# An encoder trunk whose even layer is done in two parts: seven-product pairs into DRAM, then Fourier stage and attention between the gates

## The chip, the cores and the metric

The kernel runs on one core of a Trainium2 chip. The metric is the device time of one execution in microseconds (us); smaller is better. The engines named below are PE (TensorE, matmul), DVE (VectorE), ACT (ScalarE), POOL (GpSimd) and SP (SyncE, which issues the DMAs).

## What is computed

Two requests (256 and 512 tokens, together 768) go through two layers of width 2048 in fp32. The change is in the even layer:

```python
def _even_layer(x, g, w_in, w_out, q_gain, k_gain, sink, w_f, b_f, rel_bias):
    z = _rmsnorm(x, g) @ w_in
    q, k, v, f, ga, gf = _split(z, EVEN_SPLITS)   # 1536, 512, 512, 512, 1536, 512 columns
    q = _rmsnorm(q.reshape(B, S, N_HEADS, HEAD_DIM), q_gain)       # 12 heads of 128
    k = _rmsnorm(k.reshape(B, S, N_KV_HEADS, HEAD_DIM), k_gain)    # 4 heads of 128
    v = v.reshape(B, S, N_KV_HEADS, HEAD_DIM)
    a = _window_attention(q, k, v, rel_bias, sink) * jax.nn.silu(ga)
    fo = _fourier(f.reshape(B, S, N_FOURIER, FOURIER_DIM), w_f, b_f).reshape(B, S, FOURIER_WIDTH) * jax.nn.silu(gf)
    return x + jnp.concatenate([a, fo], axis=-1) @ w_out
```

The attention sees 128-query blocks against the block before, itself and the block after; two blocks of the first request and four of the second, each with 3 query heads to one key head, make 6 units per group and 4 groups. The Fourier part is the real part of a 2-D DFT over positions and the 128 channels of a group, then a 128x128 map per group. The odd layer (short convolution and spatial gate) is not touched.

## The kernel before

All activations are kept transposed: channels on 128 partitions, the 768 tokens along the free axis, as two halves of 384. An fp32 matrix product is made from three products of high and low parts (fp32r): `three` issues hi·hi, hi·lo and lo·hi, and `split` makes the parts, a cast on ACT (line 131) and a subtraction on DVE (line 132). Inputs stand in SBUF as slots, one pair (hi, lo) per 128 channels and half.

A **block** is 128 output channels for all tokens: 16 input tiles x 2 halves x 3 = 96 matmuls of 384 columns. A **wide** step is the other way round: tokens are the output partitions and 512 output channels the columns, 288 matmuls of 512 columns for all of F. A **seven-product pair** (`strassen`) makes two blocks at once with seven half-sized products, 7 x 24 = 168 matmuls instead of 192; it needs sums of input tiles (`build_sums`) and sums of weights (lines 196 to 202, DVE), and adds results up from PSUM on DVE (lines 498 to 510). The odd layer and both output projections already use it; the even layer's input projection does not.

The even layer before: F wide; the four GF blocks (the gates of the Fourier part) with the Fourier stage between them; then four times K, three Q, V and three GA blocks (attention gates). `qk_norm` normalises a Q or K block on the spot (its sum of squares over channels is a product with a matrix of ones); the six attention units of a group (`attend`) run among the group's V and GA blocks at the times `STARTS`. At the end `load_cat` brings the 16 results back into the slots, and `Out` starts: two duos of plain blocks while the sums are built, then pairs.

PE's order is written by hand: the generators are stepped by a `Pipe` whose clock counts matmul columns, and a generator that yields a number is taken up again when that much of PE's work has been put behind it; `flush` takes up all that is left, at once and in order. The order on the other engines is the framework's, from its own estimate of times. SP's queue is in order like every engine's: a DMA that waits for its buffer holds back those behind it. `row_tile` hands out buffers of 768 columns; `Weights.ahead` loads weights (`wr`, 512 KB) some way ahead and splits them into `wh` and `wl`.

## Time and profile before

| | us |
|---|---|
| median of three runs (2163.90 to 2166.14) | 2164.87 |
| the profiled execution | 2162.2 |
| its span, first to last instruction | 2160.4 |
| PE busy in it | 2120.9 |
| F wide: 5.4 to | 89.6 |
| GF blocks and Fourier stage: to | 195.8 |
| four groups of K, Q, V, GA: to | 802.7 |
| output projection of the even layer: to | 1052.7 |

Stage ends are those of their last matmuls on PE. The four groups take 156.9 us each. The span is read with PE in mind: it is busy 98% of it, so a matmul that goes away shortens the run by its pitch, and a wait that is put on PE lengthens it.

### The profile page before, as it was taken

To read this page: it belongs to the slowest core of one execution; us is meant where nothing else is said; L and a number is where in the kernel's file an instruction comes from. 1 tells how busy PE (TensorE), PEld (TensorE's weight loads), DVE (VectorE), ACT (ScalarE), POOL (GpSimd) and SP (SyncE) were. 2 spreads that over 40 slices of the span, in tenths; PEclk is the share of its full clock that TensorE was granted. 3 is DMA by queue.
4 is the path that set the end of the run, shared out by engine and by line. 5 is a ranking of instruction groups with operands and counts; after the bars stand their busy time and mean duration, and the time that the engine had idled before them with its cause. 6 is when DMAs were issued, how large, how long until landed. Compare 5 with 4: busy or idle time off the path is not lost.

```text
span 2160.4 us, 31653 instructions
## 1 busy us (share of the span) xinstructions
PE 2120.9 (98%) x12034; PEld 2074.6 (96%) x12034; DVE 1429.5 (66%) x2466; ACT 898.9 (42%) x1761; POOL 75.0 (3%) x75
## 2 busy tenths in 40 slices
PE   7999999999999998999899999999999999999999
PEld 5899999999999998999888999999999999999999
DVE  8535755745746768666795666666666777796665
ACT  6323443443444464333544433333334554553332
POOL 5000000000000000122100000000000000000000
PEclk9999999999999999999999999999999999999999
DMA  6522112122122148344946322222222332494342
GB/s 220 145 71 77 59 65 76 50 75 66 59 66 76 49 158 275 109 137 137 312 169 194 114 72 86 86 86 76 76 76 86 105 105 97 132 305 153 119 135 74
DMA packets 116512, 250.03 MB, mean 116 GB/s; under 512 B 12636, under 2 KB 72200, under 8 KB 116360
## 3 DMA queue, kind: packets, MB, share of 16 engines
q1 hardware_dynamic: 116360, 248.01, 35.3%
q8 instruction: 94, 1.54, 0.3%
q14 instruction: 58, 0.48, 0.1%
HBM read 210.19 MB, written 40.91 MB: 116 GB/s over the span
## 4 chain that ended last, share of the span: by engine, by line
PE 90%; DVE 3%; DMA 3%; ACT 2%; issue 1%; SPq 0%; DVEq 0%; ACTq 0%
PE bank L117 89%; DMA slot<-cat 1%; PE bank L127 1%; DMA xr<-in_x_t_dram 1%; DMA s<-slot 1%; DVE slot L268 1%; DVE slot L132 1%; DVE wl L132 0%; ACT sc L730 0%; DVE slot L395 0%; DVE slot L397 0%; ACT L730 0%; ACT L350 0%; DVE slot L396 0%; DVE slot L394 0%
## 5 line engine op out<-in xcount | busy, mean ns | idle before, releaser
L117 PE MATMUL bank<-slot,wh 128*128 128x384 f32 x6848 | 1747.0, 336 | 1.3 <-DVE ev L504 1.2
L117 PEld LDWEIGHTS bank<-slot,wh 128*128 128x128 f32 x6848 | 1236.1, 188 | 2.1 <-issue 1.5
L117 PE MATMUL bank<-slot,wl 128*128 128x384 f32 x3424 | 1150.0, 336 | 8.3 <-DVE wl L132 8.3
L131 ACT CAST wh<-wr 128x512 fp32r<-128x512 f32 x728 | 447.9, 620 | 875.8 <-PE bank L117 698.7
L132 DVE TENSOR_TENSOR wl<-wr,wh 128x512 fp32r<-128x512 f32 x728 | 504.8, 697 | 364.2 <-ACT wh L131 351.5
L117 PEld LDWEIGHTS bank<-slot,wl 128*128 128x128 f32 x3424 | 643.4, 188 | 9.6 <-DVE wl L132 9.6
L117 PE MATMUL bank<-wh,slot 128*128 128x512 f32 x576 | 187.1, 403 | 11.3 <-DVE slot L268 5.9
L117 PEld LDWEIGHTS bank<-wh,slot 128*128 128x128 f32 x576 | 111.0, 193 | 37.8 <-DVE slot L268 7.6
L131 ACT CAST slot<-slot 128x384 fp32r<-128x384 f32 x176 | 87.2, 512 | 108.0 <-DVE slot L132 37.4
L132 DVE TENSOR_TENSOR slot<-slot,slot 128x384 fp32r<-128x384 f32 x176 | 97.3, 557 | 31.9 <-ACT slot L131 24.3
L117 PE MATMUL bank<-wl,slot 128*128 128x512 f32 x288 | 115.3, 401 | 1.1 <-DVE wl L132 1.1
L689 DVE RECIPROCAL nrt<-nrt 128x384 f32<-128x384 f32 x32 | 81.6, 2549 | 4.8 <-ACT nrt L688 4.8
L117 PEld LDWEIGHTS bank<-wl,slot 128*128 128x128 f32 x288 | 55.7, 193 | 13.7 <-DVE wl L132 1.6
L345 DVE TENSOR_TENSOR row<-bank,rr 128x384 f32<-128x384 f32 x40 | 22.3, 557 | 39.6 <-PE bank L117 39.6
L200 DVE TENSOR_TENSOR wr<-wr 128x1024 f32<-128x1024 f32 x36 | 47.6, 1322 | 1.2
L202 DVE TENSOR_TENSOR wr<-wr 128x1024 f32<-128x1024 f32 x36 | 44.1, 1226 | 1.2
L196 DVE TENSOR_TENSOR wr<-wr 128x1024 f32<-128x1024 f32 x36 | 44.0, 1221 | 0.5
L198 DVE TENSOR_TENSOR wr<-wr 128x1024 f32<-128x1024 f32 x36 | 43.9, 1220 | 0.4
L790 POOL TENSOR_TENSOR rr<-rr,slot 128x384 f32<-128x384 f32 x24 | 35.3, 1473 | 130.2 <-ACT slot L789 130.2
L502 DVE TENSOR_TENSOR ev<-bank,ev 128x384 f32<-128x384 f32 x36 | 20.1, 558 | 28.7 <-PE bank L117 28.7
L507 DVE TENSOR_TENSOR ev<-ev,bank 128x384 f32<-128x384 f32 x36 | 19.9, 554 | 28.6 <-PE bank L117 28.6
L268 DVE SCALAR_TENSOR_TENSOR slot<-xr,sm,slot 128x384 fp32r<-128x384 f32 x32 | 36.5, 1184 | 3.2 <-ACT slot L267 3.2
(170 smaller groups left out, 1391.6 us busy)
## 6 DMA issues: line engine op xcount, KB each, us to landing
wr<-in_w_in_o_dram SPq DMA_DIRECT2D x96, 512.0 KB, 3.7
wr<-in_w_in_e_dram SPq DMA_DIRECT2D x72, 512.0 KB, 3.7
slot<-cat SPq DMA_DIRECT2D x120, 192.0 KB, 4.2
wr<-in_w_out_e_dram SPq DMA_DIRECT2D x32, 512.0 KB, 3.9
wr<-in_w_out_o_dram SPq DMA_DIRECT2D x32, 512.0 KB, 3.9
slot<-x SPq DMA_DIRECT2D x64, 192.0 KB, 4.2
wr<-in_w_sv_dram SPq DMA_DIRECT2D x16, 512.0 KB, 4.6
xr<-in_x_t_dram SPq DMA_DIRECT2D x15, 384.0 KB, 5.5
```

Source lines behind the costliest of these rows:

```text
L117: nc.tensor.matmul(out, lhsT=lhs, rhs=rhs, start=start, stop=stop, skip_group_check=go_on)
L127: nc.tensor.transpose(out=out, in_=in_, identity=ident)
L131: nc.scalar.copy(out=hi, in_=src)
L132: nc.vector.tensor_sub(out=lo, in0=src, in1=hi.bitcast(F32))
L196: nc.vector.tensor_sub(out=w11, in0=w12, in1=w11)
L198: nc.vector.tensor_sub(out=w11, in0=w22, in1=w11)
L200: nc.vector.tensor_sub(out=w12, in0=w22, in1=w12)
L202: nc.vector.tensor_sub(out=w21, in0=w11, in1=w21)
L268: nc.vector.scalar_tensor_tensor(out=lo, in0=src, scalar=g, in1=hi.bitcast(F32), op0=ALU.mult, op1=ALU.subtract)
L345: nc.vector.tensor_mul(out=out[:, SL[s]], in0=z[s], in1=rr[:, SL[s]])
L689: nc.vector.reciprocal(out=rt, in_=rt)
L790: nc.gpsimd.tensor_add(out=rr[:, SL[h]], in0=rr[:, SL[h]], in1=sq)
```

## The change

The even layer is cut in two. **First part:** F wide as before, but its result goes to DRAM (`put_wide`, `f_d`); GF0 and GF1 as a plain duo, while `build_sums` makes the sums of the normalised inputs; V wide (16 steps, `w_vn`) to DRAM (`ve_d`), while the slots are filled with normalised inputs; then nine seven-product pairs: eight of K and Q blocks, one of GF2 and GF3. Their raw results go to DRAM (`qk_d`); the squares of each K or Q half are summed over channels by a matmul with a one-hot matrix (`pick`) into one of 16 rows of a PSUM bank that stays open for all pairs. GF gates go to DRAM too. **Second part:** the root and reciprocal of the 16 rows; the DFT tables and F are loaded (`tables`), the channel products made (`chan_mix`, before in the F stage) and the Fourier stage runs between GA0 and GA1; then 24 attention units at equal distances among GA2 to GA11. A unit loads its q from DRAM and scales it by a product of 48 rows that picks its factor (`sel`, `rstk`); the gates go through DRAM (`ga_d`). Then `load_cat` and `Out` as before, on other banks.

Over the whole program PE has 9924 matmuls of 128x384 instead of 10548, 1152 of 128x512 instead of 864, 32 new ones of 16 rows x 384 in place of 32 with `ones`, 72 new ones of 128x128 and 8 of 128x384 for `sel` (the 8 are among the 9924), and 24 transposes fewer.

```diff
+FIRST_UNIT, UNITS_AT = 14.0, 10.2
...
-        return rows[-1].tile([P, T], F32, name="row", bufs=5)
+        return rows[-1].tile([P, T], F32, name="row", bufs=4)
...
+    pick = const.tile([P, 31], F32R, name="pick")
+    nc.scalar.activation(out=pick, in_=ident[:, 0:31], func=AF.Copy, scale=0.0)
+    nc.scalar.activation(out=pick[:, 15:16], in_=ident[:, 0:1], func=AF.Copy, scale=0.0, bias=1.0)
...
+    norms = [b for g in range(NKV) for b in [K0 + g] + [Q0 + 3 * g + j for j in range(3)]]
+    pairs_in = [tuple(norms[i:i + 2]) for i in range(0, len(norms), 2)] + [(GF0 + 2, GF0 + 3)]
...
+    order += [(w_in_e, 0, GF0 + g, q) for q in range(4) for g in range(2)]
+    order += [(w_vn, "ve", 0, k) for k in KVE]
+    order += [(w_in_e, 0, b, q) for b in pairs_in for q in range(14)]
+    order += [(w_in_e, 0, GA0 + j, q) for j in range(NQ) for q in (QLATE if j == 0 else range(4))]
...
+        pipe.spawn(build_sums(normalised_x, sums, range(KH), 6.0, True), 1.0)
+        duo = (GF0, GF0 + 1)
+        st.duo(duo, (6, 7, 0, 1), None)
+        for g, b in enumerate(duo):
+            for h, z in enumerate(st.take(b)):
+                t = ev()
+                nc.vector.tensor_mul(out=t, in0=z, in1=rr[:, SL[h]])
+                nc.scalar.activation(out=t, in_=t, func=AF.Silu)
+                nc.sync.dma_start(out=gs_d[g][:, SL[h]], in_=t)
+        zv = [bank(t) for t in (2, 3, 4, 5, 0, 1)]
+        for k in KVE:
+            wide_step("ve", 0, k, zv, KVE)
+            fill(k, 0, xe_d[k][:, SL[0]])
+            fill(k, 1, s4d[k] if k < KH else xe_d[k][:, SL[1]])
+        pipe.flush()
...
+            def squares(self, i, h, t):
+                sq = big(0)
+                a, b = sq[0:64, 0:H], sq[0:64, H:T]
+                nc.scalar.activation(out=a, in_=t[0:64], func=AF.Square)
+                nc.scalar.activation(out=b, in_=t[64:P], func=AF.Square)
+                nc.vector.tensor_add(out=a, in0=a, in1=b)
+                st2 = extra(F32R)
+                nc.scalar.copy(out=st2[0:64], in_=a)
+                nc.vector.tensor_sub(out=st2[64:P], in0=a, in1=st2[0:64].bitcast(F32))
+                yield 3.5
+                mm(stat[h], pick[:, 15 - i:31 - i], st2, i + h == 0 if h == 0 else i == 1, i == 15 - h, True)
...
+        lent[0] = True
+        for b in pairs_in:
+            strassen(0, b, sums, ev, Gates() if b[0] >= GF0 else Normed(), (6, 2, 7, 3))
+        pipe.flush()
+        lent[0] = False
+        for k in range(KH):
...
+    def ga_block(j):
+        z = st.block(GA0 + j, QLATE if j == 0 else range(4))
+        g = row_tile()
+        for s in range(2):
+            nc.scalar.activation(out=g[:, SL[s]], in_=z[s], func=AF.Silu)
+        nc.sync.dma_start(out=ga_d[j], in_=g)
...
+        inv = pool.tile([16, T], F32, name="inv")
+        nc.scalar.activation(out=rstk, in_=rr[0:48], func=AF.Copy, scale=0.0)
+        for s in range(2):
+            nc.scalar.activation(out=inv[:, SL[s]], in_=stat[s], func=AF.Sqrt, bias=eps[0:16], scale=1.0 / P)
+        nc.vector.reciprocal(out=inv, in_=inv)
+        nc.scalar.copy(out=rstk[0:16], in_=inv)
+        nc.vector.tensor_sub(out=rstk[32:48], in0=inv, in1=rstk[0:16].bitcast(F32))
+
+        cwh = pool.tile([P, NF, 2 * P], F32R, name="cwh")
+        cwl = pool.tile([P, NF, 2 * P], F32R, name="cwl")
+        wf = row_tile()[:, :512]
+        nc.sync.dma_start(out=wf.rearrange("c (g d) -> c g d", g=NF), in_=w_f.rearrange("g c d -> c g d"))
+        ch = row_tile()[:, :256]
...
+        def chan_mix():
+            for f in range(NF):
+                ps = bank("s", 2 * P)
+                for j in range(2):
+                    nc.tensor.matmul(ps[:, j * P:(j + 1) * P], lhsT=ch[:, j * P:(j + 1) * P],
+                                     rhs=wf[:, f * P:(f + 1) * P], start=True, stop=True)
+                nc.scalar.copy(out=cwh[:, f, :], in_=ps)
+                nc.vector.tensor_sub(out=cwl[:, f, :], in0=ps, in1=cwh[:, f, :].bitcast(F32))
+                yield 2.0
...
+        def tables():
+            for si in (1, 0):
+                t0, nt = SEQS[si]
+                w, th, tl = tabs[si]
                     raw = row_tile()[:, :2 * w]
-                    nc.sync.dma_start(out=raw, in_=src[t])
+                    nc.sync.dma_start(out=raw, in_=(seq_p, seq_s)[si][t])
                     split(th[:, t, :], tl[:, t, :], raw)
+                    fraw = row_tile()[:, :512]
+                    nc.sync.dma_start(out=fraw, in_=f_d[t0 + t])
+                    split(*ft[t0 + t], fraw)
+                    yield 0.5
...
+        def ungated(g):
+            fo = pool.tile([P, T], F32, name="fo")
+            gf = row_tile()
+            nc.sync.dma_start(out=gf, in_=gs_d[g])
+            yield from fourier(g, fo)
+            gate(gf, NQ + g, fo)
+
+        pipe.spawn(tables(), 1.0)
+        pipe.spawn(chan_mix(), 8.0)
+        for g in range(NF):
+            pipe.spawn(ungated(g), 14.0 + 11.0 * g)
+        for j in range(2):
+            ga_block(j)
+        pipe.flush()
+        rows.pop()
...
+            qr = pool.tile([P, 3 * P], F32, name="qr", bufs=2)
+            nc.sync.dma_start(out=qr.rearrange("p (j c) -> p j c", j=3),
+                              in_=qk_d[4 * g + 1:4 * g + 4, :, t * P:(t + 1) * P].rearrange("j p c -> p j c"))
+            yield 5.0
+            ps = bank("s", 3 * P)
+            for j in range(3):
+                mm(ps[:, j * P:(j + 1) * P], gr.sel[:, j + 1, :], rstk[:, t * P:(t + 1) * P], True, True)
+            q = [pool.tile([P, 3 * P], F32R, name=f"q{e}", bufs=2) for e in "hl"]
+            scaled(qr, qg, ps, *q)
...
+            at = FIRST_UNIT + UNITS_AT * len(units) * g
+            pipe.spawn(gr.load(), max(at - 12.0, 0.0))
+            for i, (s, qb) in enumerate(units):
+                pipe.spawn(attend(gr, s, qb), at - 8.0 + UNITS_AT * i)
+        for j in range(2, NQ):
+            ga_block(j)
+        pipe.flush()
         load_cat([(k, s) for k in range(KT) for s in range(2)])
```

**Loads of tables and F, SP and DVE.** SP's queue at the loads of the DFT tables (`in_seq_p`, `in_seq_s`), in the F stage before; the names in brackets are what a row waits for:

```order
50 L595 DMA row<-in_seq_p_dram 128x260 [waits DMAHW1_49]
51 L595 DMA row<-in_seq_p_dram 128x260 [waits DMAHW2_49]
52 L595 DMA row<-in_seq_s_dram 128x516 [waits DMAHW3_49]
53 L595 DMA row<-in_seq_s_dram 128x516 [waits DMAHW4_49,PE_49]
54 L595 DMA row<-in_seq_s_dram 128x516 [waits DMAHW5_49]
55 L595 DMA row<-in_seq_s_dram 128x516 [waits DMAHW6_49,DMAHW1_49,DVE_49]
56 L184 DMA wr<-in_w_in_e_dram 128x1024 [waits DMAHW7_49]
57 L184 DMA wr<-in_w_in_e_dram 128x1024 [waits DMAHW0_49,DVE_49]
```

and after, where they stand behind the pairs; `f_d` is F, `in_w_in_e` weights:

```order
264 L734 DMA row<-in_seq_s_dram 128x516 [waits DMAHW1_49]
265 L737 DMA row<-f_d 128x512 [waits DMAHW2_49]
266 L734 DMA row<-in_seq_s_dram 128x516 [waits DMAHW3_49,DMAHW1_49,DVE_49]
267 L737 DMA row<-f_d 128x512 [waits DMAHW4_49,DMAHW2_49,DVE_49]
268 L191 DMA wr<-in_w_in_e_dram 128x1024 [waits DMAHW5_49,DVE_49]
269 L734 DMA row<-in_seq_s_dram 128x516 [waits DMAHW6_49,DMAHW3_49,DVE_49]
270 L737 DMA row<-f_d 128x512 [waits DMAHW7_49,DMAHW4_49,DVE_49]
271 L734 DMA row<-in_seq_s_dram 128x516 [waits DMAHW6_49,DMAHW0_49,DVE_49]
272 L737 DMA row<-f_d 128x512 [waits DMAHW7_49,DVE_49]
273 L734 DMA row<-in_seq_p_dram 128x260 [waits DMAHW0_49,DVE_49]
274 L737 DMA row<-f_d 128x512 [waits DMAHW1_49,DVE_49]
```

VectorE there after (`tl` and `fl` are the low parts of tables and F, `inv` the 16 rows' reciprocal):

```order
472 L699 RECIPROCAL inv<-inv 16x768 [waits Activation_49]
473 L134 TENSOR_TENSOR tl_4568<-row,th_4567 128x516 [waits DMAHW1_49,Activation_49]
474 L134 TENSOR_TENSOR fl_4574<-row,fh_4573 128x512 [waits DMAHW2_49,Activation_49]
475 L701 TENSOR_TENSOR rstk<-inv,rstk 16x768 [waits DMAHW5_49,DMAHW4_49,Activation_49]
476 L134 TENSOR_TENSOR wl<-wr,wh 128x512 [waits PE_49] x2
477 L717 TENSOR_TENSOR cwl<-bank,cwh 128x256 [waits PE_49]
478 L717 TENSOR_TENSOR cwl<-bank,cwh 128x256 [waits Activation_49]
479 L134 TENSOR_TENSOR tl_4568<-row,th_4567 128x516 [waits DMAHW3_49,Activation_49]
480 L134 TENSOR_TENSOR fl_4576<-row,fh_4575 128x512 [waits DMAHW4_49,Activation_49]
```

Two loads went out without a wait for DVE; from the third on each load waits for the subtraction that frees its buffer, with the reciprocal ahead of the first.

**Squares of a pair's results, DVE.** Before (`qk_norm`, `sc` is a copy of the bank; line 680 adds the squares):

```order
135 L676 TENSOR_TENSOR sc<-bank,rr 128x384 [waits DMAHW3_49,DMAHW5_49,DMAHW0_49,DMAHW6_49,DVE_49,PE_49]
136 L680 TENSOR_TENSOR sc<-sc,nsq 64x384 [waits Activation_49]
137 L676 TENSOR_TENSOR sc<-bank,rr 128x384 [waits PE_49]
138 L132 TENSOR_TENSOR wl<-wr,wh 128x512 [waits Activation_49]
139 L683 TENSOR_TENSOR pth<-sc,pth 64x384 [waits Activation_49]
140 L680 TENSOR_TENSOR sc<-sc,nsq 64x384 [waits Activation_49]
141 L683 TENSOR_TENSOR pth<-sc,pth 64x384 [waits Activation_49]
```

After, the last two halves of a pair; lines 203, 205 and 207 are sums of weights, 632 and 635 the sum of squares and its low part, 512 a result from PSUM:

```order
226 L203 TENSOR_TENSOR wr<-wr 128x1024 [waits DMAHW3_49,DMAHW2_49,DMAHW5_49,DMAHW1_49,DMAHW6_49,DMAHW0_49,DVE_49]
227 L632 TENSOR_TENSOR big_2181<-big_2181 64x384 [waits Activation_49]
228 L207 TENSOR_TENSOR wr<-wr 128x1024 [waits DMAHW6_49,DVE_49]
229 L635 TENSOR_TENSOR slot_2185<-big_2181,slot_2185 64x384 [waits PE_49,Activation_49]
230 L134 TENSOR_TENSOR wl<-wr,wh 128x512 [waits PE_49]
231 L512 TENSOR_TENSOR ev<-bank,ev 128x384 [waits PE_49]
232 L134 TENSOR_TENSOR wl<-wr,wh 128x512 [waits Activation_49]
233 L205 TENSOR_TENSOR wr<-wr 128x1024 [waits DVE_49]
234 L632 TENSOR_TENSOR big_2224<-big_2224 64x384 [waits Activation_49]
235 L134 TENSOR_TENSOR wl<-wr,wh 128x512 [waits PE_49,Activation_49]
236 L635 TENSOR_TENSOR slot_2228<-big_2224,slot_2228 64x384 [waits Activation_49]
```

What stood in a row among weight splits now stands among sums of weights as well.

**End of the attention, PE.** Before, the last unit's product with V (`pth`, `ptl`) is followed by blocks of the group's gates (`slot`):

```order
4190 L117 MATMUL bank<-slot_339,wh 128x384
4191 L117 MATMUL bank<-slot_338,wl 128x384
4192 L117 MATMUL bank<-pth,vh 128x384
4193 L117 MATMUL bank<-ptl,vh 128x384
4194 L117 MATMUL bank<-pth,vl 128x384
4195 L117 MATMUL bank<-pth,vh 128x384
4196 L117 MATMUL bank<-ptl,vh 128x384
4197 L117 MATMUL bank<-pth,vl 128x384
4198 L117 MATMUL bank<-slot_377,wh 128x384
4199 L117 MATMUL bank<-slot_378,wh 128x384
4200 L117 MATMUL bank<-slot_377,wl 128x384
4201 L117 MATMUL bank<-slot_416,wh 128x384
```

After, in the flush, the last unit's scores:

```order
4031 L119 MATMUL bank<-rstk,sel 128x128 x3
4032 L119 MATMUL bank<-kh,qh 128x256
4033 L119 MATMUL bank<-kl,qh 128x256
4034 L119 MATMUL bank<-kh,ql 128x256
4035 L119 MATMUL bank<-kh,qh 128x256
4036 L119 MATMUL bank<-kl,qh 128x256
4037 L119 MATMUL bank<-kh,ql 128x256
4038 L119 MATMUL bank<-kh,qh 128x256
4039 L119 MATMUL bank<-kl,qh 128x256
4040 L119 MATMUL bank<-kh,ql 128x256
4041 L119 MATMUL bank<-pth,vh 128x384
4042 L119 MATMUL bank<-ptl,vh 128x384
```

and the flush's end, where the `slot` rows are already the output projection's:

```order
4047 L119 MATMUL bank<-pth,vh 128x384
4048 L119 MATMUL bank<-ptl,vh 128x384
4049 L119 MATMUL bank<-pth,vl 128x384
4050 L129 MATMUL bank<-ident,sc 128x128 x6
4051 L119 MATMUL bank<-pth,vh 128x384
4052 L119 MATMUL bank<-ptl,vh 128x384
4053 L119 MATMUL bank<-pth,vl 128x384
4054 L119 MATMUL bank<-pth,vh 128x384
4055 L119 MATMUL bank<-ptl,vh 128x384
4056 L119 MATMUL bank<-pth,vl 128x384
4057 L119 MATMUL bank<-slot_8255,wh 128x384
4058 L119 MATMUL bank<-slot_8256,wh 128x384
```

The rows of three units now stand in a row, with no block between a unit's scores (`kh`, `qh`), its transposes (`ident`) and its product with V.

## Rows read from the trace of the kernel before

**Rows 1.** The page: busy time of each engine, and the chain that ended last.
```profile
PE 2120.9 (98%) x12034; PEld 2074.6 (96%) x12034; DVE 1429.5 (66%) x2466; ACT 898.9 (42%) x1761; POOL 75.0 (3%) x75
PE 90%; DVE 3%; DMA 3%; ACT 2%; issue 1%; SPq 0%; DVEq 0%; ACTq 0%
```

**Rows 2.** What TensorE waited for over the whole span (releaser: total us, times, longest).
```profile
PE bank L117 <- DVE wl L132: 9.4, 5, 3.1
PE bank L561 <- DVE cwl L564: 6.7, 1, 6.7
PE bank L127 <- DVE sc L736: 6.0, 4, 1.5
```

**Rows 3.** Windows: start:end and length, then busy (x count) per engine, clock, DMA share, GB/s.
```profile
1300.00:1400.00 100.00, 100.00 (x577) 100.00 (x576) 63.96 (x98) 32.93 (x57) 0.17 (x3) 1.00 0.26 87
1100.00:1140.00 40.00, 40.00 (x175) 32.47 (x174) 35.92 (x71) 18.12 (x35) 0.00 (x0) 1.00 0.57 197
45.40:52.50 7.10, 0.40 (x3) 0.07 (x1) 7.10 (x7) 3.71 (x8) 4.64 (x3) 0.81 0.29 90
803.00:844.00 41.00, 41.00 (x238) 41.00 (x237) 37.70 (x75) 20.09 (x42) 0.32 (x1) 1.00 0.88 292
```

**Rows 4.** Instructions grouped by line and shape: busy us, mean ns, idle before.
```profile
L131 ACT CAST wh<-wr 128x512 fp32r<-128x512 f32 x728 | 447.9, 620 | 875.8 <-PE bank L117 698.7
L132 DVE TENSOR_TENSOR wl<-wr,wh 128x512 fp32r<-128x512 f32 x728 | 504.8, 697 | 364.2 <-ACT wh L131 351.5
L131 ACT CAST slot<-slot 128x384 fp32r<-128x384 f32 x176 | 87.2, 512 | 108.0 <-DVE slot L132 37.4
L132 DVE TENSOR_TENSOR slot<-slot,slot 128x384 fp32r<-128x384 f32 x176 | 97.3, 557 | 31.9 <-ACT slot L131 24.3 <-DMA s<-slot 5.7
L689 DVE RECIPROCAL nrt<-nrt 128x384 f32<-128x384 f32 x32 | 81.6, 2549 | 4.8 <-ACT nrt L688 4.8
L680 DVE TENSOR_TENSOR sc<-sc,nsq 64x384 f32<-64x384 f32 x32 | 17.6, 550 | 25.6 <-ACT nsq L679 16.1 <-ACT sc L678 9.5
L200 DVE TENSOR_TENSOR wr<-wr 128x1024 f32<-128x1024 f32 x36 | 47.6, 1322 | 1.2
```

**Rows 5.** DMA issues: count, KB each, median us from issue to landing.
```profile
slot<-cat SPq DMA_DIRECT2D x120, 192.0 KB, 4.2
slot<-xhat SPq DMA_DIRECT2D x24, 192.0 KB, 2.5
row<-in_seq_s_dram SPq DMA_DIRECT2D x4, 258.0 KB, 5.2
row<-in_w_f_dram SPq DMA_DIRECT2D x1, 256.0 KB, 3.7
```

**Rows 6.** Timeline of VectorE, one attention unit: scores' end to scaled scores.
```profile
755.13 0.56 DVE L719 CUSTOM_DVE_ANT_0 sc<-bank,bias 128x384 f32<-128x384 f32 x1
756.60 0.17 DVE L727 TENSOR_SCALAR nm<-nm 128x3 f32<-128x3 f32 x1
759.74 0.17 DVE L734 RECIPROCAL den<-den 128x3 f32<-128x3 f32 x1
760.27 1.07 DVE L736 TENSOR_SCALAR sc<-sc,den 128x384 f32<-128x384 f32 x3
```

**Rows 7.** Timeline of TensorE around the channel products of the Fourier branch.
```profile
45.35 0.39 PE L117 MATMUL bank<-wh,slot 128*128 128x512 f32 x1
52.44 1.22 PE L561 MATMUL bank<-row 128*128 128x128 f32 x4 [6.70 <-DVE cwl L564]
53.31 0.77 PE L117 MATMUL bank<-wh,slot 128*128 128x512 f32 x1
```

**Rows 8.** Timeline of ScalarE, a change of activation table and back.
```profile
766.29 0.85 ACT L350 ACTIVATE row<-row 128x768 f32<-128x768 f32 x1
767.14 1.28 ACT L730 ACT_TABLE_LOAD   x1
768.43 0.51 ACT L730 ACTIVATE sc<-sc,nm 128x256 f32<-128x256 f32 x1
```

More of the change, by code (lines that the diff above doesn't have):

```diff
@@ L381, in big, with build_sums @@
     def big(i, dtype=F32):
[L382 to L384 removed]
+        return late[-1].tile([P, PW], dtype, name=f"big{i}")
+    def build_sums(load, sums, order, every, own=False):
         for j in order:
```

483 lines of the change are left out of this document (242 added, 241 removed).

## The prediction

> **What bounds the kernel now.** I read the page first: PE is busy 98% of the span of 2160.4 us and carries 90% of the chain that ended last [rows 1]. So the run is PE's matmuls plus the few places where PE waits, and I need two counts: how many matmuls the change takes away at which pitch, and which waits go or come. The pitch is read from full stretches: in the odd layer's seven-product pairs 577 matmuls of 384 columns in 100 us, 0.174 us each once the two cut by the edges are taken off; in the odd layer's wide step 175 of 512 columns in 40 us, 0.231 [rows 3]. Narrower ones I take in proportion, 0.045 per 100 columns, as an estimate. The waits of PE in the part that changes are few: 6.7 us at the channel products in the F stage, 6.0 in four waits of transposes for scaled scores (the last unit of each of the four groups), and the larger part of 9.4 for weight splits, in the first duos of the output projection [rows 2]. The profiled execution took 2162.2, its span 2160.4; the median of the runs, 2164.87, is 2.7 above it. I make the sum against the profiled one and put it on the median.
>
> **What goes.** Nine pairs by seven products save 9 x 24 = 216 matmuls: -37.6. V as a wide step is 288 x 0.231 = 66.5 for 384 x 0.174 = 66.8: -0.3. 24 transposes fewer, -1.4. The 32 sums of squares with 16 rows stand for 32 with ones: nothing. Scaling q and k by products adds 72 x 0.058 + 8 x 0.174 = +5.6. PE's own work: -33.7.
>
> Three waits go too. In the F stage PE stood from 45.74 to 52.44 for the channel products [rows 7] while VectorE was busy 7.10 of 7.10 us [rows 3], then ran on at a clock of 0.81 in that stretch; they now stand elsewhere. 6.7, the last product's own 0.87 (52.44 to 53.31), and 0.8 for matmuls at the low clock behind it: -8.4 (-6, if the inputs' own splits are late next, to -10). The four waits for scaled scores: -6.0; the tails they stood in no longer exist. In the output projection the weight splits waited because VectorE, 37.7 of 41 us busy there [rows 3], still had to split the 16 results; after the change most of those splits fall into the wait that I find below, so I take -4 of the 6 us of that place (0 to -6). In all -52.1.
>
> **What comes, the Fourier stage.** `row_tile` has four buffers here; `w_f` and `chan` hold two until the channel products are done, so tables and F have one pair of buffers, and six pairs of loads go through it one after another, each waiting for the subtraction of the pair before, as SP's rows show. A turn is a load of 3.7 us (256 KB, little else in flight), a cast 0.62 and a subtraction 0.70 [rows 4, 5]: 5.05 with the hand-over. The first turn ends late: on VectorE the reciprocal of 768 columns, 2 x 2.55 = 5.1 [rows 4], stands ahead of its subtractions, and ahead of that the eight refills of slots, which can be loaded only when the last pair has read them, 4.2 for a load and 8 x 0.56 for the subtractions [rows 4, 5], with a root and its table load on ScalarE some 10.2 us after the last pair's end. So the reciprocal ends at 15.3, the first turn at 16.7, the sixth at 16.7 + 5 x 5.05 = 42. PE comes to the first Fourier product after some 16 us of GA0 and would need 3.6 for its 30 products; it is held until 42: **+22** (16 if a load takes the 2.5 us that the lightest of its kind, `xhat`, took, 29 if it takes the 5.2 that `seq_s` took in a crowded stretch [rows 5]). All of GA0 and GA1 stands behind in PE's queue, so nothing covers it. The fourth Fourier piece runs in the flush, +1.
>
> The Trainium skill, "DMA: Bandwidth & Descriptors", section "Anatomy of one DMA", puts a transfer at 2.0 us plus its bytes at 436 GB/s, 2.6 for 256 KB; by that five turns would cost 5 us less. The rows have 3.7 for this size on SP's queue, and I go by them.
>
> **What comes, the tail of the attention.** After GA11's last matmul a softmax is running and three units have not scored. Their chain is laid bare: from the last score to scaled scores 5.7 us in the trace (755.69 to 761.34 [rows 6]); transposes 1, cast and subtraction 1.1, product with V 1.6. I walked the queues from that matmul: first unit's transposes at 1.9 (slot refills stand between on VectorE); the second scores till 5.6, its q being split first; ScalarE then has eight casts for refills, 8 x 0.51 [rows 4], a copy, a weight cast and a table load ahead of the exponentials, so it is scaled at 14.8; the third's q is cast behind those exponentials, it scores till 15.0 and is scaled at 22.2; PE's order has the second unit's product with V behind the third's transposes, 24.8, and the factors for the last unit's q behind that, so it scores till 27.8, is scaled at 31.6 and done at 34. PE has 13.2 us of work in it: **+21** (14 to 25).
>
> The Trainium skill, "ScalarE: Activation LUTs", section "What ACT_TABLE_LOAD costs", counts 1.28 us and a drain of 1.38 for a switch; two of them here would make the tail 2.8 longer. In the trace the next ACTIVATE starts 0.01 us after the load's 1.28 and the load right at the end of the one before [rows 8], so no drain is added.
>
> **What comes, small waits.** A pair's squares: two adds from PSUM, two squares, an add, a cast and a subtraction, some 4.6 us by durations of 0.5 to 0.56 each [rows 4], for a matmul put 3.5 us of the Pipe's clock (4.3 us by the pitch and the tick) behind; with a weight sum in the way it is late for some halves: +3 (0 to 12). Duo and V with VectorE about 80% busy and 290 GB/s of DMA: the stretch 803 to 844 ran at 92% and 292 GB/s without a wait [rows 3]: +1 (0 to 8). Attention between the gates: a unit of three blocks has 7.0 us for a chain of 5.7 to 7.2: +3 (0 to 10). Matmuls at the low clock behind the two long waits: the one after 6.7 us was 0.57 us from its successor instead of 0.23 [rows 7] and a few like it, in five or six places: +3.
>
> The sum: -52.1 + 22 + 1 + 21 + 3 + 1 + 3 + 3 = +1.9, 2164.1 for the profiled execution, 2166 or 2167 for a median. I say **2166**: what PE saves in matmuls it gives back in two waits.
>
> **The rivals.** *The two waits are half as long.* For it: both hang on queue orders that I walked by hand, loads have been seen at 2.5 us [rows 5], and refills land in any order; against it, SP's rows leave no second buffer. Turns of 4 us, near the 2.5, give 37 instead of 42 (-5), a tail without the refills' casts ahead of the exponentials 26 (-8), and small waits of 5 instead of 10: 2148. By the skill's price for a transfer the first of these alone would hold, 2161. Without either wait it would be 2121, which the orders exclude almost wholly.
>
> *The squares hold up every pair* (slower). For it: two sums of weights of 1.3 us [rows 4] stand among the squares on VectorE, and the stat matmul stands in PE's queue with the pair's products behind it. It decides from a chain of 4.3 us on: with one sum ahead it is 5.9, a wait of 1.6; twice in each of eight pairs is 25 instead of 3, and the chance of once is as large: 2178 to 2188. Against it, `qk_norm` before, with the same 3.5 but without the two adds in front, shows no wait in [rows 2].
>
> *Loads crowd the Fourier stage* (slower): turns of 6.5 give 49, +7, and units in the attention wait 0.4 each, +7: 2180.
>
> *The seven products save nothing* since VectorE becomes the bound in the pairs: it was 64% busy in the odd layer's pairs with PE full [rows 3]; the squares add some 5 points. Under 3%.
>
> **How the numbers follow.** Forecast 40% (its own range 2157 to 2175), half-length waits 27%, squares 16%, crowded loads 14%, others 3%. A measurement of this kernel tells some 0.2%, 4.3 us, from no change: faster means below 2160.5, slower above 2169.2. The first rival gives 27 and the forecast's low end 8: 35% faster. The forecast's high end gives 9, the slow rivals 28: 37% slower. The rest, 28%, is the same. For 8 in 10 the range takes in the first rival's price and most of the slow ones: 2147 to 2184.
>
> **What would show it.** In the profile after: F's last matmul near 81; PE full in the pairs, with small waits for the subtraction of the squares; a wait of some 22 us at the first Fourier product, released by casts and subtractions of tables and F in turn, 5 us apart; 24 units with next to no wait; 34 us from GA11's end to the output projection, with PE busy for 13; fewer waits for weight splits behind it. Wrong would be: tables that land in pairs without waiting for one another, squares that hold up every pair, or a tail in which ScalarE takes the exponentials ahead of the refills.

## The result

The changed kernel takes 2180.72 us (median of four, 2175.53 to 2182.72) where the kernel before, on the same chip, takes 2165.34: a ratio of 1.0068, 95% interval 1.0049 to 1.0087. It is slower by 15 us; the forecast was 2166, its range 2147 to 2184. The profiled execution took 2179.42, its span is 2177.6, against 2162.2 and 2160.4.

What answers to [rows 1], the busy time and the chain that ended last, on the page of the changed kernel:

```profile
PE 2121.1 (97%) x11778; PEld 2038.8 (94%) x11778; DVE 1486.3 (68%) x2628; ACT 977.2 (45%) x1907; POOL 75.0 (3%) x75
...
PE 83%; DVE 8%; DMA 3%; ACT 3%; issue 2%; SPq 0%; POOL 0%; ACTq 0%; DVEq 0%
```

PE has fewer matmuls and is busy just as long, 2121.1 against 2120.9: some of what is left runs slower. And the chain goes over VectorE for 8% instead of 3%. What PE waited for, as in [rows 2] (releaser: total us, times, longest):

```profile
PE bank L119 <- ACT fh L133: 10.3, 4, 3.8
PE bank L119 <- DVE slot L635: 8.3, 16, 0.8
PE bank L119 <- DVE slot L277: 7.3, 2, 5.9
PE bank L119 <- ACT qh L133: 7.1, 3, 4.3
...
PE bank L119 <- ACT slot L276: 5.2, 1, 5.2
PE bank L129 <- DVE sc L894: 5.1, 2, 4.3
```

The wait for the channel products is gone (line 561 before). New are the Fourier stage (`fh`), the squares (line 635, in 16 places) and the tail of the attention (`qh`, `sc`). The lines 276 and 277 are the inputs of the first stages of both layers, which the kernel before has too. Stages by windows (columns as in [rows 3]): F; duo and V; eight pairs, up to the last product of the squares; first Fourier piece with a channel product; tail; output projection:

```profile
5.22:78.98 73.76, 71.90 (x307) 57.73 (x307) 58.16 (x60) 43.87 (x78) 31.19 (x15) 1.00 0.75 213
78.98:177.61 98.63, 98.63 (x482) 87.38 (x480) 76.79 (x145) 44.95 (x89) 0.00 (x0) 1.00 0.85 286
177.61:434.20 256.59, 247.44 (x1401) 238.36 (x1399) 172.23 (x256) 128.86 (x236) 0.00 (x0) 1.00 0.32 101
...
477.12:497.06 19.94, 9.48 (x36) 7.30 (x35) 7.44 (x14) 7.12 (x14) 0.00 (x0) 0.62 0.45 136
...
786.22:824.04 37.82, 25.07 (x97) 21.02 (x97) 25.82 (x77) 20.55 (x53) 0.00 (x0) 0.72 0.30 97
824.04:1071.20 247.16, 244.91 (x1393) 244.13 (x1393) 168.06 (x256) 109.40 (x203) 40.09 (x29) 0.99 0.56 180
```

Put against the steps of the prediction (times of the profiled executions, new minus old):

| step | forecast | measured | from |
|---|---|---|---|
| matmuls, without the factors' products | -39.3 | -39.3 | counted at the forecast's pitch, not measured |
| products that pick the factors | +5.6 | about +19 | 0.69 a group of three, 0.57 a product of 384 columns by itself |
| F stage | -8.4 | -10.5 | 73.8 against 84.3 |
| duo and V | +1 | -1.3 | 98.6 against 99.9 of matmuls |
| squares of the pairs | +3 | +13.2 | 24 of 32 places: 16 late by 0.61 to 0.92, eight by some 0.27 |
| Fourier stage | +23 | +17.4 | 19.2 instead of 3.6, and 1.8 at channel products |
| tail, with its low clock | +24 | +24.6 | 37.8 with 13.2 of work |
| waits of the old tails | -6.0 | -6.0 | gone |
| output projection and odd layer | -4 | -4.1 | 1353.6 against 1357.7 behind its first matmul |
| attention between the gates | +3 | +4 | what is left of the sum |
| sum | +1.9 | +17.2 | spans |

Two rows carry the miss: the factors' products and the squares, 24 us together; the Fourier stage gave back 6 and the first stages 4. The sum fits its range because these partly cancel.

The tail went nearly as it was walked. TensorE's timeline there (start, length, engine, line, instruction, count, idle before and releaser):

```profile
786.69 1.15 PE L129 MATMUL bank<-ident,sc 128*128 128x128 f32 x6
788.93 0.62 PE L119 MATMUL bank<-kh,qh 128*128 128x384 f32 x1 [1.09 <-ACT qh L133]
...
798.21 0.69 PE L119 MATMUL bank<-kh,qh 128*128 128x384 f32 x1 [4.32 <-ACT qh L133]
...
801.52 1.72 PE L129 MATMUL bank<-ident,sc 128*128 128x128 f32 x9
807.53 2.41 PE L129 MATMUL bank<-ident,sc 128*128 128x128 f32 x9 [4.30 <-DVE sc L894]
...
815.10 0.38 PE L119 MATMUL bank<-kh,qh 128*128 128x256 f32 x1 [1.74 <-ACT qh L133]
...
824.04 0.84 PE L119 MATMUL bank<-slot,wh 128*128 128x384 f32 x2
```

Transposes, scores, scores and two lots of transposes in a row, most of them waiting for the step before. Between 798.21 and 801.52 nine matmuls of 384 columns stand 0.37 apart, the last ones 0.32 instead of 0.174: the granted clock of the tail's window is 0.72, and PE had been idle for 4 us ahead of them. The waits listed for the tail are 12.5 us (`qh` 7.1, `sc` 5.1, `pth` 0.3). PE takes the other 25.3 for work of 13.2 us at full pace, so half of the tail's cost, 12 us, is slow matmuls and not waiting.

### The profile page after: what moved, and what is told of

It reads as the page before. It is cut to its first block, busy times and chain, and to the rows that moved or that the text cites. A ratio compares the mean times of both kernels' runs of the same rounds, so it can differ in the third digit from the quotient of the medians.

```text
span 2177.6 us, 32105 instructions
## 1 busy us (share of the span) xinstructions
PE 2121.1 (97%) x11778; PEld 2038.8 (94%) x11778; DVE 1486.3 (68%) x2628; ACT 977.2 (45%) x1907; POOL 75.0 (3%) x75
## 4 chain that ended last, share of the span: by engine, by line
PE 83%; DVE 8%; DMA 3%; ACT 3%; issue 2%; SPq 0%; POOL 0%; ACTq 0%; DVEq 0%
PE bank L119 82%; DVE wl L134 2%; DVE slot L277 1%; PE bank L129 1%; DMA slot<-cat 1%; ACT wh L133 1%; DVE slot L134 1%; DVE slot L635 1%; DVE wr L205 0%; DVE wr L207 0%; ACT sc L888 0%; DMA slot<-x 0%; DMA s<-slot 0%; DMA x<-ev 0%; ACT slot L133 0%
## 5 line engine op out<-in xcount | busy, mean ns | idle before, releaser
L119 PE MATMUL bank<-slot,wh 128*128 128x384 f32 x6448 | 1651.0, 337 | 0.8 <-DVE ev L506 0.8
L119 PEld LDWEIGHTS bank<-slot,wh 128*128 128x128 f32 x6448 | 1164.2, 188 | 4.2 <-issue 2.0
L119 PE MATMUL bank<-slot,wl 128*128 128x384 f32 x3224 | 1084.2, 336 | 3.6 <-DVE wl L134 3.5
L134 DVE TENSOR_TENSOR wl<-wr,wh 128x512 fp32r<-128x512 f32 x782 | 541.4, 696 | 349.4 <-ACT wh L133 329.8
L119 PEld LDWEIGHTS bank<-slot,wl 128*128 128x128 f32 x3224 | 606.5, 188 | 4.6 <-DVE wl L134 4.6
L119 PE MATMUL bank<-wh,slot 128*128 128x512 f32 x768 | 243.9, 397 | 12.5 <-DVE slot L277 7.3
L119 PEld LDWEIGHTS bank<-wh,slot 128*128 128x128 f32 x768 | 145.9, 190 | 46.0 <-DVE slot L277 9.0
L119 PE MATMUL bank<-wl,slot 128*128 128x512 f32 x384 | 152.2, 396 | 1.9 <-DVE wl L134 1.9
L134 DVE TENSOR_TENSOR slot<-slot,slot 128x384 fp32r<-128x384 f32 x232 | 127.8, 556 | 37.8 <-ACT slot L133 32.0
L207 DVE TENSOR_TENSOR wr<-wr 128x1024 f32<-128x1024 f32 x45 | 58.4, 1299 | 1.2
L209 DVE TENSOR_TENSOR wr<-wr 128x1024 f32<-128x1024 f32 x45 | 55.1, 1225 | 1.5
L203 DVE TENSOR_TENSOR wr<-wr 128x1024 f32<-128x1024 f32 x45 | 55.0, 1221 | 0.8
L205 DVE TENSOR_TENSOR wr<-wr 128x1024 f32<-128x1024 f32 x45 | 54.9, 1221 | 0.7
L888 ACT ACTIVATE sc<-sc,nm 128x256 f32<-128x256 f32 (+1 forms) x72 | 38.3, 533 | 0.4 <-DVE nm L885 0.3
```

What stands on the lines that cost most here:

```text
L119: nc.tensor.matmul(out, lhsT=lhs, rhs=rhs, start=start, stop=stop, skip_group_check=go_on)
L134: nc.vector.tensor_sub(out=lo, in0=src, in1=hi.bitcast(F32))
L203: nc.vector.tensor_sub(out=w11, in0=w12, in1=w11)
L205: nc.vector.tensor_sub(out=w11, in0=w22, in1=w11)
L207: nc.vector.tensor_sub(out=w12, in0=w22, in1=w12)
L209: nc.vector.tensor_sub(out=w21, in0=w11, in1=w21)
```

## The experiments

Each is the changed kernel (the last three the kernel before) with the edit shown. Times are compared by ratios to the kernel before on the same chip; a difference of 0.001 is 2.2 us. The intervals of the first, second and changed kernel overlap, so for edits of 5 us the stage that was edited is the better witness. Stage times are those of the profiled execution; what an edit doesn't touch varies too: from the end of the even layer's output projection to the end of the run it is 1106 to 1110 us in the changed kernel and the four single edits.

**The squares put later.**

```diff
-                yield 3.5
+                yield 5.0
                 mm(stat[h], pick[:, 15 - i:31 - i], st2, ...)
```

> The products that sum the squares are put 5.0 instead of 3.5 of the Pipe's clock behind their squares (33 instead of 24 matmuls). Theory: their chain of ACT and DVE steps is about 0.7 us too long for 24 matmuls in two of the four halves of a pair; the changed kernel's trace has 13 us of it in 31 such places, so this version is 9 to 12 us faster than the changed kernel, and the waits of the matmul for the subtraction in line 635 are gone. Rival: what stands there is the price of going from 128 output rows to 16 on PE, not a wait; then nothing changes (within 2 us), and the places keep their 0.6 us.

Ratio 1.0044 (1.0028 to 1.0061), some 5 us less than the changed kernel's 1.0068, where 9 to 12 were expected; the pairs' stage takes 249.4 instead of 256.6, with six more matmuls (1 us) ahead of its end. VectorE and ScalarE in the changed kernel at one of those places, and PE waiting there (two additions of results, from 198.65, and the first square stand ahead of these rows):

```profile
201.48 0.55 DVE L632 TENSOR_TENSOR big<-big 64x384 f32<-64x384 f32 x1 [1.19 <-ACT big L631]
202.12 0.69 DVE L134 TENSOR_TENSOR wl<-wr,wh 128x512 fp32r<-128x512 f32 x1
202.84 0.55 DVE L635 TENSOR_TENSOR slot<-big,slot 64x384 fp32r<-64x384 f32 x1
```

```profile
200.92 0.52 ACT L631 ACTIVATE big<-ev 64x384 f32<-64x384 f32 x1
201.47 0.62 ACT L133 CAST wh<-wr 128x512 fp32r<-128x512 f32 x1
202.06 0.52 ACT L634 CAST slot<-big 64x384 fp32r<-64x384 f32 x1
```

```profile
203.45 0.35 PE L119 MATMUL bank<-slot,pick 128*16 128x384 f32 x1 [0.47 <-DVE slot L635]
```

The chain is DVE (two additions), ACT, ACT (the squares), DVE (their sum), ACT, DVE (its high and low part), with two weights' subtractions and a cast in it, 198.65 to 203.4: 4.7 us where 24 matmuls take 4.2. This is the second of a pair's four halves. The first is on time, within 0.02 us, the third late by some 0.27 and the fourth by 0.69 to 0.72. In the third and the fourth a sum of weights does stand ahead of the squares' sum on VectorE; the fourth:

```profile
241.38 1.22 DVE L205 TENSOR_TENSOR wr<-wr 128x1024 f32<-128x1024 f32 x1
242.53 0.55 DVE L632 TENSOR_TENSOR big<-big 64x384 f32<-64x384 f32 x1
```

In the experiment the second half's product has 30 matmuls ahead of it (5.0 gives 33 in the first half of a pair, 30 in the others), and PE goes through:

```profile
203.59 0.34 PE L119 MATMUL bank<-slot,wl 128*128 128x384 f32 x1
203.76 0.34 PE L119 MATMUL bank<-slot,pick 128*16 128x384 f32 x1
203.94 0.51 PE L119 MATMUL bank<-slot,wh 128*128 128x384 f32 x2
```

0.17 ahead of the 16-row product and 0.18 behind it: going to 16 output rows costs nothing that can be seen, and the rival is out. Of the 16 waits 8 are left, 3.2 us in the list: those of the fourth half, still late by 0.54 or more. By the products' starts the lateness fell from 13.2 us to 4.7, just under the 9 expected for that reason.

**128 rows for the factors.**

```diff
-    rstk = mid.tile([48, T], F32R, name="rstk")
+    rstk = mid.tile([P, T], F32R, name="rstk")
...
-                self.sel = pool.tile([48, 4, P], F32R, name="sel", bufs=2)
+                self.sel = pool.tile([P, 4, P], F32R, name="sel", bufs=2)
```

The 80 rows more are zero.

> The products that pick the factors of q and k get 128 contraction rows (80 of them zero) instead of 48. Theory: in the changed kernel's trace a group of three of them costs 0.6 us instead of the 0.17 of my sum, because PE pauses at each change between 128 and 48 rows (0.27 before, 0.20 behind, 0.28 for the next but one); with 128 rows throughout 24 groups lose 0.3 to 0.45 each: 7 to 11 us faster than the changed kernel. Rival: the cost is that of any three short products with their own weights; then the groups keep their 0.6 us and the time stays within 2 us.

Ratio 1.0043 (1.0028 to 1.0058): 5 us less, where 7 to 11 were expected; the stretch from the last Fourier piece to the last gate block takes 247.0 instead of 254.1. The products for k, of 384 columns like their neighbours, show the change of rows by itself. With 48 rows, then with 128:

```profile
541.62 0.44 PE L119 MATMUL bank<-rstk,sel 48*128 48x384 f32 x1
541.98 0.62 PE L119 MATMUL bank<-slot,wh 128*128 128x384 f32 x2
```

```profile
543.93 0.33 PE L119 MATMUL bank<-rstk,sel 128*128 128x384 f32 x1
544.10 0.51 PE L119 MATMUL bank<-slot,wh 128*128 128x384 f32 x2
```

The ordinary matmul ahead starts 0.27 before the first product and 0.18 before the second, the next one 0.37 and 0.17 behind. Up to the third ordinary one it is 0.57 for the product with 48 rows and 0.18 with 128: the change of rows costs 0.39. TensorE's timeline around one group of three, with 48 rows:

```profile
602.32 0.55 PE L119 MATMUL bank<-rstk,sel 48*128 48x128 f32 x3
602.80 0.62 PE L119 MATMUL bank<-slot,wh 128*128 128x384 f32 x2
603.26 0.35 PE L119 MATMUL bank<-slot,wl 128*128 128x384 f32 x1
```

and with 128:

```profile
602.12 0.45 PE L119 MATMUL bank<-rstk,sel 128*128 128x128 f32 x3
602.40 0.56 PE L119 MATMUL bank<-slot,wh 128*128 128x384 f32 x2
602.79 0.34 PE L119 MATMUL bank<-slot,wl 128*128 128x384 f32 x1
```

Each piece stands behind one more ordinary matmul, which starts at 602.05 with 48 rows and at 601.94 with 128. From there to the start of the last row shown is 1.21 us with 48 rows, where the three ordinary matmuls alone would take 0.52: 0.69 a group. With 128 rows it is 0.85, so 0.33 a group. Of the 0.69 the change of rows takes 0.36 (0.10 ahead of the group, some 0.2 behind its last, the rest in the two after). Of the other 0.33 the columns as priced are 0.17; short products cost the rest beyond their columns: 0.28 for three, and 0.05 more for the next. So both the theory and the rival have a part in it. No wait stands in these rows, so the list of waits can't show it; the starts do. In the whole stretch PE's busy time fell by 8.8 us (253.6 to 244.8), and 1.8 came back as small waits for attention units.

**Two pairs of buffers for tables and F.**

```diff
-        inv = pool.tile([16, T], F32, name="inv")
+        inv = row_tile()[0:16]
...
-                    raw = row_tile()[:, :2 * w]
+                    raw = pool.tile([P, TS + 4], F32, name="raw", bufs=2)[:, :2 * w]
...
-                    fraw = row_tile()[:, :512]
+                    fraw = pool.tile([P, 512], F32, name="fraw", bufs=2)
```

The channel products' two inputs share one row buffer, of which there are three here.

> Tables and F get two pairs of load buffers instead of one (the small inputs share a row, the row of the reciprocal is one of three row buffers). Theory: the first Fourier piece, 19.2 us instead of 3.6, is held by the loads going one pair after another, 4 to 5 us a turn; with two in flight it takes 8 to 11 and the whole is 8 to 11 us faster than the changed kernel. Rival: the reciprocal and the refills of the slots ahead of it on VectorE, or the DMA rate, hold it; then it keeps 16 us or more and the time moves by less than 3 us.

Ratio 1.0030 (1.0018 to 1.0041): 8 us less, as expected; the first Fourier piece and the channel product behind it take 9.5 instead of 19.9. SP's timeline in the changed kernel shows the turns (the loads of the tables; one of F follows each):

```profile
464.89 0.33 SPq L734 DMA_DIRECT2D row<-in_seq_s_dram  x1
...
473.05 0.33 SPq L734 DMA_DIRECT2D row<-in_seq_s_dram  x1
...
489.27 0.33 SPq L734 DMA_DIRECT2D row<-in_seq_p_dram  x1
```

The first, the second and the last of six stand here: 8.2 us for the first turn, held by the reciprocal (467.54 to 472.48 on VectorE), then 16.2 for four, 4.1 each. In the experiment two pairs go out at 465.17 to 466.58, and PE waits 1.1 us at most. The theory holds.

**Units 9.6 apart.**

```diff
-FIRST_UNIT, UNITS_AT = 14.0, 10.2
+FIRST_UNIT, UNITS_AT = 14.0, 9.6
```

> The attention units stand 9.6 instead of 10.2 apart, so that the last begins 14 us earlier. Theory: the tail behind the last gate block, 37 us with 13 us of work in it, is softmax chains with no block between them; with one or two units left in it instead of three it takes 15 to 22 us, and the whole is 12 to 18 us faster than the changed kernel, if the 24 units find their chains in time at the closer spacing. Rival: the tail is set by the refills of the slots for the output projection, which can be loaded only behind the last gate block; then 25 us or more remain between that block and the output projection, and the gain is under 6 us.

Ratio 1.0031 (1.0018 to 1.0044): 8 us less, where 12 to 18 were expected. The tail takes 14.2 instead of 37.8, and the stretch of gates 265.1 instead of 254.1, since two units' matmuls now stand in it: 12.6 less for both together; in this execution the stretches that the edit doesn't touch took some 4 us longer. Gates and tail:

```profile
798.81:813.02 14.21, 8.51 (x39) 6.83 (x40) 10.53 (x30) 10.16 (x23) 0.00 (x0) 0.83 0.32 112
533.76:798.81 265.05, 262.99 (x1555) 249.39 (x1554) 173.73 (x511) 167.71 (x381) 0.00 (x0) 1.00 0.43 140
```

What the tail lacked was cover; the rival, that refills set it and 25 us or more stay, is out.

**All four.**

The four edits above in one kernel, with the squares later still:

```diff
-                yield 5.0
+                yield 6.0
```

> The four edits together: the sums of squares 6.0 of the Pipe's clock behind, 128 rows for the factors, two pairs of load buffers for tables and F, units 9.6 apart. Theory: the four losses stand in four stages of PE's row and add up; by the stages of the four traces they are worth 7 to 10, 7, 10 and 13 us, so this is 35 to 40 us faster than the changed kernel and 1.0 to 1.3% faster than the kernel before. Rival: what one edit frees is given back at the next wait (the closer units need VectorE where the factors' chain ran late, the loads start earlier into the refills); then it is less than 25 us faster than the changed kernel and within 0.5% of the kernel before.

2135.26 us, ratio 0.9886 (0.9871 to 0.9901): 39 us less than the changed kernel, 25 less than the kernel before (2160.84 on that chip). By stages 10.8 in the pairs (with 12 more matmuls, 2.1 us, ahead of the stage's end), 10.9 in the first Fourier piece, 21.8 in gates and tail. The losses add up at least, as they stand in different stages of one row of matmuls: by the profiled spans the four edits give 10.5, 9.3, 7.5 and 8.4 us one by one, 36 in all, and 44 together, of which some 5 are from the squares' last move, which takes the lateness left from 4.7 to 0. By the ratios it is 27 one by one and 39 together; each of the four carries the changed kernel's own interval of 4 us, so the difference is not explained further. The window of the pairs:

```profile
177.69:423.53 245.84, 245.84 (x1412) 243.21 (x1411) 171.87 (x254) 128.54 (x234) 0.00 (x0) 1.00 0.32 104
```

The pairs run without a wait now, with VectorE busy 172 of 246 us: the seven products do save what they should.

**Fourier pieces later.**

```diff
-            pipe.spawn(ungated(g), 14.0 + 11.0 * g)
+            pipe.spawn(ungated(g), 20.0 + 9.0 * g)
```

on top of all four.

> As e5_all, with the four Fourier pieces at 20, 29, 38 and 47 instead of 14, 25, 36 and 47 of the Pipe's clock, so that more of GA0 stands ahead of the first. Theory: of the first piece's 9.5 us with two pairs of buffers some 6 are still waiting for loads; 6 us more of gate matmuls ahead hide 4 to 6 of it: 4 to 6 us faster than e5_all. Rival: the pieces come closer to one another and to the flush, and wait for their own casts; then it is within 2 us of e5_all.

2128.88, ratio 0.9853 (0.9836 to 0.9869): 7 us less than with the four edits, where 4 to 6 were expected. The first piece takes 3.60 us, its bare matmuls; the channel product that waited behind it has moved ahead too.

**Units 9.2 apart.**

```diff
-FIRST_UNIT, UNITS_AT = 14.0, 9.6
+FIRST_UNIT, UNITS_AT = 14.0, 9.2
```

on top of that.

> As e6_all_f20, with the units 9.2 instead of 9.6 apart. Theory: the 14.2 us that are left between the last gate block and the output projection still hold 6 us of scores and transposes and 7 of waits for the last two units; 9 us earlier only the last unit's product with V is left there, 3 to 6 us, and what PE does there moves among the gate blocks: 4 to 8 us faster than e6_all_f20. Rival: at 9.2 the chains of the units no longer end in time and PE waits a little in each of 24 units: within 2 us of e6_all_f20 or slower.

2121.56, ratio 0.9828 (0.9790 to 0.9867): the fastest, 1.7% ahead of the kernel before and, by the two ratios, 2.4% ahead of the changed one. Against the version at 9.6 the intervals overlap; in the profiles the span falls from 2127.2 to 2118.5. From the last gate block to the output projection 1.7 instead of 14.2 is left, while the output projection itself takes 251.3 instead of 246.1: about 5 of the 12.6 us come back, in one wait for a weight's subtraction, which stands behind splits and sums of refilled slots on VectorE:

```profile
810.69 0.69 PE L121 MATMUL bank<-slot,wl 128*128 128x384 f32 x1 [7.37 <-DVE wl L136]
```

At 9.6 the longest such wait there is 2.0. This is the opposite of what the tail had done for the output projection.

**The channel products out of the F stage of the kernel before.** One part of the change alone.

```diff
+                if g == 0:
+                    pipe.spawn(chan_mix())
                 pipe.spawn(fourier(g, fo), 6.0)
```

`chan_mix` is the loop over the four products, cut out of `prep`.

> The kernel before, with the channel products alone moved out of the F stage, to the beginning of GF0. Theory: the F stage loses its wait of 6.7 us, the products' own matmuls and the low clock behind: 84 us become 74, as in the changed kernel, and since GF0 takes the products without a wait the run is 7 to 10 us faster than before. Rival: PE then runs into the inputs' splits, which the wait had let run ahead, or GF0 waits for the products; then it is within 3 us of the kernel before.

2165.58, ratio 1.0021 (1.0012 to 1.0031): not the 7 to 10 us faster that were expected but slightly slower, and the F stage 86.4 us instead of 84.3. The wait in [rows 7] is gone and others have come, at the stage's end:

```profile
77.70 0.80 PE L117 MATMUL bank<-wh,slot 128*128 128x512 f32 x1 [3.27 <-ACT wh L131]
...
84.91 2.72 PE L117 MATMUL bank<-ones,rs 128*128 128x2 f32 x12 [2.62 <-ACT rr L281]
```

ScalarE's timeline tells why:

```profile
75.53 0.75 ACT L131 CAST th<-row 128x260 fp32r<-128x260 f32 x2 [15.96 <-DMA row<-in_seq_p_dram]
76.51 0.62 ACT L131 CAST th<-row 128x516 fp32r<-128x516 f32 x1 [0.23 <-DMA row<-in_seq_s_dram]
77.04 0.61 ACT L131 CAST wh<-wr 128x512 fp32r<-128x512 f32 x1
```

It stands 16 us at the cast of a table, whose load went out at 68 us behind the twelve bias writes, and a weight's cast stands behind. In the kernel before PE came to that matmul 10 us later (at 84.1; here it stood from 74.4 to 77.7) and met nothing. My explanation of the F stage's gain was incomplete.

**The tables moved too**, first only in the code's order:

```diff
+            def tables():
+                for si in (1, 0):
...
+                    pipe.spawn(tables(), 0.5)
-                pipe.spawn(fourier(g, fo), 6.0)
+                pipe.spawn(fourier(g, fo), 6.0 if g else 12.0)
```

> The kernel before with two things moved out of the F stage: the channel products, as in b1_chan_later, and the loads of the DFT tables, to the beginning of GF0; the first Fourier piece stands 12 instead of 6 of the Pipe's clock behind the beginning of GF0. Theory, from the trace of b1_chan_later: with the products alone moved the F stage kept its 86 us, because the tables' loads land late behind the bias writes and their casts stand ahead of weight casts on ScalarE; with both away the F stage takes 74 to 76 us as in the changed kernel, and the run is 6 to 10 us faster than the kernel before, if the first Fourier piece doesn't wait for the tables. Rival: the F stage is held by its inputs whatever stands in it; then it keeps 82 us or more and the run is within 3 us of the kernel before.

2167.16, ratio 1.0023 (1.0011 to 1.0035), the F stage 87.0 us; 6 to 10 us less were expected. This told nothing apart: nothing kept the loads and casts from their old place, and the framework's order left them there (the first cast at 76.14, behind 17.5 us of idle ScalarE). Then with buffers whose memory comes free only behind the stage:

```diff
-                        raw = row_tile()[:, :2 * w]
+                        raw = fpool[0].tile([P, TS + 4], F32, name="raw", bufs=2)[:, :2 * w]
```

> As b2_tables_too, where the framework's order had kept the loads and casts of the tables in the F stage after all (ScalarE cast them from 76 us on, between the weights); here they are loaded into buffers whose memory comes free only behind that stage, so that their casts stand behind F's own. Theory: the F stage of b1 and b2 was held by those casts, which wait for loads queued behind the twelve bias writes; without them it takes 74 to 76 us instead of 84, as in the changed kernel. Then the first Fourier piece may wait some 2 to 5 us for the tables, and the run is 4 to 9 us faster than the kernel before. Rival: the F stage is held by something else that the channel products only hid; it keeps 82 us or more and the run is no faster than the kernel before.

2151.29, ratio 0.9952 (0.9936 to 0.9969): 10 us faster than the kernel before, a little more than the 4 to 9 expected. The F stage takes 73.85, as in the changed kernel, and ScalarE has the tables' casts behind F's own:

```profile
77.44 3.57 ACT L616 ACTIVATE fh<-bank,rt 128x512 fp32r<-128x512 f32 x6 [0.26 <-DVE rt L292]
...
81.39 1.19 ACT L131 CAST th<-raw 128x516 fp32r<-128x516 f32 x2
```

So the F stage's 10 us in the changed kernel come from two moves together, and that of the channel products alone was worth nothing; the tables' move alone wasn't run. The kernel before gets this 0.5% without its even layer cut in two: of the 1.7% of the fastest version some 1.2 are left for the rest of the change.

## Why the prediction was right, and where it was not

The range held the time, at its upper part; the likeliest case, no change, did not come, and the chances of faster and slower had been nearly even (35 and 37%). That the sum came within 15 us is in part luck: two terms were 24 us too small together, others 10 too large. The idea of it held in part: what the matmuls save is given back, but only some of it in waits; the rest is PE at a slower pace, in the factors' products and in the tail. The four added losses (factors, squares, Fourier stage, tail) measured 74 us; the four edits take 39 of them out again and leave a kernel 1% faster than before.

**The waits that go.** The F stage measured -10.5 for -8.4 (-6 to -10). The number was nearly right for an incomplete reason: the tables' casts were not in the step at all, although their loads stood in the SP rows of the change's description. The inputs' own splits were named as what may be late next; late next, with the products moved alone, was the cast of a table. The waits of the old tails are gone, and PE's waits for weights' subtractions are 4.0 less over the run (5.4 for 9.4), as forecast.

**The Fourier stage.** Mechanism as told: turns, the reciprocal ahead of the first, PE held. The term was 23 and measured 17.4. Counted from the last pair's end at 459.4, the reciprocal was done at 13.1 us (15.3 walked), the first turn at 14.2 (16.7) and the sixth at 36.5 (42), so 2.5 us are the earlier start and 3 the turns, 4.5 on average instead of 5.05. PE came to the first Fourier product after 17.7 us instead of 16, which takes another 1.7 off. The loads landed in 2.8 us (F) and 3.1 (`seq_s`), by the list of DMA issues of the changed kernel:

```profile
row<-f_d SPq DMA_DIRECT2D x6, 256.0 KB, 2.8
...
row<-in_seq_s_dram SPq DMA_DIRECT2D x4, 258.0 KB, 3.1
```

I had taken 3.7, from a load in the crowded first stage. The estimate of 2.6 from the Trainium skill ("DMA: Bandwidth & Descriptors", "Anatomy of one DMA — SWDGE (gpsimd) path") was nearer here than my row. But the page measured its fit on DMAs that GpSimd issues, which the prediction did not say, and these loads go out on SP's queue. So the nearness is no test of the fit, and of the 5 us that it would have taken off the turns show 3.

**The tail.** Forecast 34 us, and 3 for the low clock here and at the other long wait; measured 37.8. Counted from GA11's last matmul, the third unit scored till 15.3 us (15.0 walked) and was scaled at 21.3 (22.2), and the last unit scored till 30.7 (27.8). Walking three queues by hand with durations from the trace gave this to 10%. The make-up was off: the forecast had 21 us of waits and 3 of low clock, the trace has 12.5 of waits and 12 of slow matmuls. Behind the third unit's scaled scores, its transposes and the second unit's products with V took 5.2 us (807.5 to 812.7) instead of 2.6. How much of the slow work would have been waiting at full pace, no run shows. The switch of ScalarE's table cost 1.28 us and nothing behind it, as in [rows 8] (load at 794.46, next instruction at 795.76). The 1380 ns of drain that the Trainium skill adds to a load ("ScalarE: Activation LUTs", "What ACT_TABLE_LOAD costs") does not show here.

**The factors' products.** The step that failed: I priced them by columns, 0.058 each, 5.6 in all; they cost 19. Two things were missing, and the experiment with 128 rows separates them: going from 128 to 48 rows and back, 0.36 us a group, and short products that don't reach the pace of their columns, 0.09 a matmul instead of 0.058 and a slower start behind them. The trace before had rows to show the second (its transposes of 128 columns stand some 0.11 apart, nine in 1.14 us) and none for the first. The Trainium skill states something that may be the first, "TensorEngine Tiling (Array Packing)", "Key Properties": changing the tiling mode drains TensorE. The rows with 48 contraction rows agree with that, though the trace doesn't name the mode; for the 16 output rows of the squares' product they show no such pause. I had not weighed it.

**The squares.** Forecast +3 with 0 to 12 allowed and a rival of 25; measured 13.2, between them. The chain was worked out as 4.6 us and is 4.7 in a pair's second half; what failed is the price. The forecast's own figures had the chain longer than its room of 4.3 us, in every half, and booked +3 for "some halves" only; 0.3 in 32 places would have been 10. The room was 24 matmuls, 4.17 us. The rival was right that two halves of each pair are held up, though by 0.65 us and not 1.6, and half right on the cause: a sum of weights stands in the chain of the fourth half, two subtractions of weights in that of the second.

**Small terms.** Duo and V ran without any wait at 286 GB/s and 78% of VectorE. The attention between the gates cost 4 instead of 3 beside the factors.

## What to carry to other kernels

A chain that has to meet PE at a point needs room for one more step of each queue it passes, and the room must be counted in matmuls as the trace paces them; 0.6 to 0.9 us too little, 16 times, was 11 of the 13 us that the squares cost. A wait that is taken away uncovers the next thing in the same queue: look at which in-order queue stood idle during the old wait, and what stood at its head. And losses that stand in different stretches of one engine's row add up when they are removed: four edits that gave 27 us one by one by the ratios, 36 by the profiled spans, gave 39 and 44 together.

## What the hardware showed that was not expected

- A group of three matmuls of 48 rows x 128 columns among matmuls of 128 rows takes 0.69 us more than none, 0.33 with 128 rows; one of 48 rows x 384 columns by itself takes 0.57, 0.18 with 128 rows. The squares' products with 16 output rows (128 x 16, 384 columns) take 0.18 like any of 384 columns. Small products are not cheap by their size on PE.
- Behind a group of 48 rows the next ordinary matmul starts 0.20 after the last `sel`, and the two from there take 0.46 instead of 0.35; with 128 rows it is 0.11 and 0.39.
- PE's clock falls to its lower level (1.2 GHz) in the tail, the first time already behind the wait of 1.09 us ahead of 788.93 (granted 0.52 from there to 791.98): 0.32 us for 384 columns in most of the stretch, granted clock 0.72 for the 37.8 us. With the tail gone, and the Fourier stage covered, the granted clock of the whole run rises from 0.988 to 0.997. That is part of what the experiments gained: in the tail, 12.5 us of waits came with 12 us of slower matmuls.
